# Output projection of a hybrid decoder layer: which block runs token-major, and in which order the blocks go

## The chip, the cores and the metric

One core of a Trainium2 chip. The metric is the device time of one execution in microseconds, the median of several runs. TensorE (PE, its weight loads PEld), VectorE (DVE), ScalarE (ACT), GpSimd (POOL) and SyncE (SP, which issues every DMA of this kernel) run side by side.

## The reference, cut to what matters

```
x: 2048 prompt tokens and 8 decode tokens, 2048 channels, float32
h    = RMSNorm(x) * (1 + scale) + shift
P    = h @ w_in                          -> u_a | v_a | z_a | x_b | z_b
y_a  = u_a * (tril(W_s) LN(v_a) + b_s) * SiLU(z_a)
y_b  = GLU(S5 state space of x_b) * SiLU(z_b)
o    = concat(y_a, y_b) @ w_out          (2048 x 2048)
out  = x + gate * RMSNorm(o) * g_post    (gate differs for prompt and decode rows)
```

The change touches the last two lines alone. RMSNorm needs the sum of squares over all 2048 channels of `o` before any output can be written.

## The kernel before, in words

Matrix products are made of three matmuls on float32r halves: each operand is split into a high and a low part (`split`, L87: a cast on ScalarE, L90, and a subtraction, L85), and high x high, low x high and high x low are summed in PSUM. Each matmul loads its own 128 x 128 stationary operand.

The 2056 tokens are four blocks of 512, the last with the 8 decode rows (`blk`). The input projection runs in two parts; in part two the order is block 3, 0, 1, 2. It leaves `y` in DRAM (`YA[b][h]`, by block, and `YB[e]`, by group of channels). Then comes the output projection, the subject here. Its stages are:

- `phase3` (L1137), channel-major, for blocks 0, 1 and 2: W_out is stationary, `y` (128 channels x 512 tokens) streams. There are 16 tiles of 128 output channels (n), each a sum over 16 row tiles (k). The first ng = 4 tiles share one pass over k, in which the `y` rows that aren't there yet are loaded (`yload`, L1085, six ahead; rows 8 to 15 come from `YB` in pieces of 256 bytes and are cast at L1098); then n = 4 to 15 one by one, with the next tile's W_out loaded meanwhile. `ev_o` (L1105) takes a finished tile out of PSUM: its square goes to a running sum (GpSimd, L1121), its value times the gate to SBUF.
- `phase3` for block 3, channel-major for its tokens 256 to 511 and the decode rows only: 264 columns per matmul, ng = 6.
- `phase3_rows` (L1228), token-major, for tokens 0 to 255 of block 3: `y` is stationary, W_out (128 x 512) streams; four quarters f of 512 channels, in each 16 k and two token tiles c. Here a token lies on a partition, so the sum of squares is per partition, and a token tile can be scaled as soon as it is complete. In the last quarter tile 1 runs LAG = 6 steps of k behind tile 0, so that tile 0's ending lies beside matmuls.

So W_out (16.8 MB) is read five times, each time in 32 pieces of 512 KB (`wraw`, L106), each split into two pairs of halves; `phase3_rows` asks for a piece four pieces ahead (`rows_w`, L1224).

The ending of a channel-major block (`final`, L1189) needs a sum over partitions (`rms_wide`, two matmuls with a matrix of ones), a reciprocal root on VectorE, and for each of 16 tiles a load of the residual (L1196, four buffers), a product (L1206), a sum (L1207) and a store (L1208). It is a generator: `finish_some` runs a step of it at given places of the next stage (k = 11, 13 and 15 of the first group, then once per tile). `gg_rows` (L1211) makes the gate as rows for the token-major stage: four activations and, in a later `turn`, a float32 matmul and a copy, four times; in block 3's channel-major part after n = 6, 8, 10 and 12. The token-major ending (`final` inside `phase3_rows`, L1237) is a chain of short VectorE instructions on 128 x 1 to the scale, then per quarter a fused multiply-add with the residual `xr` (L1254), one of the four on ScalarE and GpSimd instead (L1251, L1252), and a store (L1255).

All instructions are traced in written order; the framework then orders each engine's queue by priority and a simulated timeline, so transfers may be issued ahead of their written place, as far as buffers are free. `hl` has 32 buffers (16 rows of y, high and low), raw rows `t` six, raw pieces of W_out three, `o` tiles OB = 21.

Of the kernel before, what the change touches and what calls it, by code (L numbers as in the profile page):

```python
# [19 lines left out]
D = 2048  # L20
L = 2048
ND = 8
# [23 lines left out]
OB = 21  # L46
LAG = 6
NR_ = 8
XR0 = 41
OW = 2 * (TB // 2 + ND)  # L50

# [11 lines left out]
class Builder:  # L63
# [1041 lines left out]
    def ev_o(self, b, n, acc, rs, ssq, eng):  # L1105
        S, V = self.S, self.V
        if b < NB - 1 or n % 2 == 0:
            self.o2 = self.xp.tile([128, OW], F32, tag="o", bufs=OB, name=self.nm("o"))
        o = self.o2[:, n % 2 * (OW // 2) :] if b == NB - 1 else self.o2
# [12 lines left out]
        return o  # L1122
# [13 lines left out]

    def phase3(self, b, ws, y):  # L1137

        V, G, SP = self.V, self.G, self.SP
        rs = ranges(b) if b < NB - 1 else ranges(b)[1:]  # L1140
        c0 = rs[0][0]
        nn = rs[-1][0] + rs[-1][1] - c0
        ng = 4 if b < NB - 1 else 6
        ssq = self.xp.tile([128, TB + ND], F32, tag="ssq", bufs=2, name=self.nm("ossq"))
        kw = [{}, self.wkw]
        ws = [ws]
        acc = [[self.ps.tile([128, 512], F32, tag="acc" if g < 4 else "aux", bufs=4, name=self.nm("acc"))] for g in range(ng)]
# [12 lines left out]
        for g in range(ng):  # L1160
            self.finish_some(1)
            os_.append(self.ev_o(b, g, acc[g], rs, ssq, G))
        for n in range(ng, 16):
            ac = [self.ps.tile([128, 512], F32, tag="acc", bufs=4, name=self.nm("acc")) for _ in rs]
            nxt = []
            for k in range(KT):
                if k % 8 == 0 and n < 15:
                    nxt += self.wsplit(self.whalf(self.I["wout"][n + 1], k // 8), **(self.wkw if k else {}))
                self.kstep(ac, w, k, y[k], rs, k == 0, k == KT - 1)
                if k == 13:  # L1170
                    self.run_later()
                if n == 15 and b < NB - 1:
                    if k >= 4 and k % 2 == 0:
                        ynext.append(self.yload(b + 1, len(ynext)))
                    if k in (1, 9) or (k == 13 and b == NB - 2):
                        g = len(wnext)
                        wnext.extend(self.wsplit(self.wpair(self.I["wout"], g, 0), **kw[g // 4]))
                elif n == 15 and k in (1, 9):
                    wnext.append(self.rows_w(len(wnext)))
            self.finish_some(1 if n < 15 or b == NB - 1 else 16)  # L1180
            if b == NB - 1 and n % 2 == 0 and 6 <= n < 14:
                self.gg_rows((n - 6) // 2)
            os_.append(self.ev_o(b, n, ac, rs, ssq, G))
            w = nxt
        self.finish_some(16)
        self.finish = self.final(ssq, nn, os_, b * TB + c0, b * TB)
        return (y if b == NB - 1 else ynext), wnext

# [39 lines left out]
    def phase3_rows(self, b, y, ws):  # L1228

        V, G, S, T, SP = self.V, self.G, self.S, self.T, self.SP  # L1230
        ssq = self.sp_.tile([128, 2, 4], F32, name="ssqr")
        ws = dict(enumerate(ws))
        for i in range(len(ws), 4):
            ws[i] = self.rows_w(i)
        os_, xs = {}, {}
        mm = T.matmul
        def final(c):  # L1237

# [6 lines left out]
            self.rsqrt(r, v, t, h)  # L1245
            if c:
                V.tensor_mul(os_[c, 3], acc[c], self.ggr[3])
            for f in range(4):
                o, x = os_[c, f], xs[c, f]
                if f == 1 - c:  # L1250
                    S.activation(o, o, AF.Identity, scale=r)  # L1251
                    G.tensor_tensor(o, o, x, op=ALU.add)  # L1252
                else:
                    V.scalar_tensor_tensor(o, o, r, x, op0=ALU.mult, op1=ALU.add)  # L1254
                SP.dma_start(self.O["yr"][c * 128 : c * 128 + 128, f * 512 : f * 512 + 512], o)  # L1255
        for f in range(4):
            acc = [self.ps.tile([128, 512], F32, tag="acc", bufs=4, name=self.nm("acc")) for _ in range(2)]
            lag = LAG if f == 3 else 0
            held = []
            for k in range(KT + lag):  # L1260
                i = f * 8 + k // 2
                if k < KT and k % 2 == 0:
                    held += ws.pop(i)
                for c, kc in ((0, k), (1, k - lag)):
                    if not 0 <= kc < KT:
# [4 lines left out]
                    mm(acc[c], yh, wh, start=kc == 0, stop=False)  # L1270
                    mm(acc[c], yl, wh, start=False, stop=False)
                    mm(acc[c], yh, wl, start=False, stop=kc == KT - 1)
                    if kc == KT - 1:
                        sq = self.xp.tile([128, TB + ND], F32, tag="sq", bufs=2, name=self.nm("osq"))[:, 0:512]
                        os_[c, f] = self.xp.tile([128, OW], F32, tag="o", bufs=OB, name=self.nm("or"))[:, 0:512]
                        S.activation(sq, acc[c], AF.Square, accum_out=ssq[:, c, f : f + 1])
                        if (c, f) != (1, 3):
# [3 lines left out]
                if k < KT and k % 2:  # L1281
                    if i + 4 < 32:
                        ws[i + 4] = self.rows_w(i + 4)
                    if f or k >= 13:
                        self.finish_some(1)
                    if f * 16 + k >= XR0 and len(xs) < 8:
                        c, g = len(xs) // 4, len(xs) % 4
                        x = self.xp.tile([128, OW], F32, tag="o", bufs=OB, name=self.nm("xr"))[:, 0:512]
                        SP.dma_start(x, self.I["xr"][c][:, g * 512 : g * 512 + 512])
                        xs[c, g] = x  # L1290

# [85 lines left out]
    def build(self):  # L1377
# [108 lines left out]
        for b in (NB - 1, *range(NB - 1)):  # L1486
# [4 lines left out]
            else:  # L1491
                y0, ws0 = [], []
                raws = []
                def last(k):

                    if k == 1:
                        raws.extend(self.wraw(self.wpair(I["wout"], g, 0)) for g in (0, 2))
                    if k in (9, 14):
                        ws0.extend(self.wpieces(raws.pop(0)))
# [29 lines left out]
def layout(i):  # L1529
# [17 lines left out]
    out["woutr"] = i["w_out"].reshape(KT, 128, 4, 512).transpose(2, 1, 0, 3)  # L1547
    out["xr"] = x[(NB - 1) * TB : (NB - 1) * TB + NR].reshape(2, 128, D)
    out["ident"] = np.eye(128, dtype=np.float32)
# [23 lines left out]

NR = 256
OUTS = {"yT": (D, T - NR), "yr": (NR, D), "sav": (128, H, ND), "hp": (128, 2, 32), "hs": (128, 2, 32, ND)}


def unpack(r):
    t0 = (NB - 1) * TB
    yT = r["yT"].T  # L1580
# [16 lines left out]
```

## Time and profile before

| | |
|---|---|
| median of 3 runs | 2885.63 us (2882.94 to 2888.16) |
| profiled execution, device time | 2882.97 us |
| its span, first to last instruction | 2880.9 us |
| TensorE busy | 2817.2 us (98%), 15708 matmuls |
| weight loads / VectorE / ScalarE / GpSimd busy | 82% / 55% / 37% / 36% |
| DMA | 581.20 MB, 202 GB/s over the span |

A TensorE row's duration includes the passage through the array, so its pace is read from starts. Busy times are per stretch; `x` counts instructions that touch the stretch.

### The profile page before, as it was taken

What the parts mean: (1) busy time and instruction counts of PE and PEld (TensorE: products, weight loads), DVE (VectorE), ACT (ScalarE), POOL (GpSimd) and SP (SyncE); (2) the same over time, 40 slices, a digit from 0 to 9 for tenths busy, and PEclk for the clock granted to TensorE, in tenths of its full rate; (3) what the DMA queues carried; (4) which work ended last, traced back from release to release, by engine and by line L of the source; (5) the groups of instructions that cost most, each with busy time, mean ns of one, the idle gap of its engine ahead of it and who ended that gap; (6) DMA issues with size and microseconds to landing.
All of it is one profiled execution on the core that took longest, in us unless ns stands there. A gap on an engine that the chain in (4) does not pass through costs nothing.

```text
span 2880.9 us, 44125 instructions
## 1 busy us (share of the span) xinstructions
PE 2817.2 (98%) x15708; PEld 2365.8 (82%) x15708; DVE 1570.4 (55%) x2907; ACT 1062.2 (37%) x2008; POOL 1048.5 (36%) x973
## 2 busy tenths in 40 slices
PE   7999999999999999999999999999999999999998
PEld 4676777778899999988888888888888888888976
DVE  4467656465342837564647545573641273472866
ACT  3334444334233232423233332433243333434543
POOL 1128562662431233323232323233334355263442
PEclk9999999999999999999999999999999999999999
DMA  9898997987987373847475656646573355464676
GB/s 363 287 250 230 265 261 229 282 234 210 198 209 207 106 236 125 267 131 223 133 245 185 180 174 196 209 145 208 159 229 106 112 178 171 132 219 126 197 235 221
DMA packets 455167, 581.20 MB, mean 202 GB/s; under 512 B 216609, under 2 KB 303265, under 8 KB 454945
## 3 DMA queue, kind: packets, MB, share of 16 engines
q1 hardware_dynamic: 454946, 578.38, 66.9%
q8 instruction: 123, 2.02, 0.3%
q14 instruction: 98, 0.80, 0.1%
HBM read 466.94 MB, written 102.66 MB: 198 GB/s over the span
## 4 chain that ended last, share of the span: by engine, by line
PE 73%; DVE 14%; DMA 6%; issue 3%; POOL 1%; SPq 1%; ACT 1%; DVEq 0%; ACTq 0%; POOLq 0%
PE acc L97 21%; PE acc L99 20%; PE acc L98 20%; DVE Ub L943 3%; DVE wlo L85 2%; PE acc L655 2%; PE acc L656 2%; PE acc L657 2%; PE ada L271 1%; DMA wraw<-in_win 1%; DVE Ub L954 1%; DVE sct L953 1%; DVE sct L951 1%; DVE Ub L952 1%; DMA wraw<-in_woutr 1%
## 5 line engine op out<-in xcount | busy, mean ns | idle before, releaser
L85 DVE TENSOR_TENSOR wlo<-wraw,whi 128x512 fp32r<-128x512 f32 x626 | 544.6, 878 | 832.9 <-ACT whi L90 811.8
L90 ACT CAST whi<-wraw 128x512 fp32r<-128x512 f32 x960 | 580.4, 620 | 1101.3 <-PE acc L98 634.8
L97 PE MATMUL acc<-hi,whi 128*128 128x512 f32 (+2 forms) x2816 | 979.2, 349 | 1.4 <-ACT vtok L663 0.8
L99 PE MATMUL acc<-hi,wlo 128*128 128x512 f32 (+2 forms) x2816 | 968.7, 344 | 4.0 <-DVE wlo L85 3.9
L98 PE MATMUL acc<-lo,whi 128*128 128x512 f32 (+2 forms) x2816 | 968.2, 344 | 3.8 <-DVE lo L375 3.5
L85 POOL TENSOR_TENSOR wlo<-wraw,whi 128x512 fp32r<-128x512 f32 x334 | 472.7, 1418 | 1025.0 <-ACT whi L90 911.8
L97 PEld LDWEIGHTS acc<-hi,whi 128*128 128x128 f32 x2816 | 531.1, 189 | 82.2 <-issue 14.0
L99 PEld LDWEIGHTS acc<-hi,wlo 128*128 128x128 f32 x2816 | 530.4, 188 | 74.0 <-DVE wlo L85 6.1
L98 PEld LDWEIGHTS acc<-lo,whi 128*128 128x128 f32 x2816 | 531.1, 189 | 65.0 <-DVE lo L375 6.7
L97 PE MATMUL acc<-yhi,whi 128*128 128x512 f32 (+1 forms) x1024 | 377.3, 369 | 3.8 <-DVE o L1118 2.8
L99 PE MATMUL acc<-yhi,wlo 128*128 128x512 f32 (+1 forms) x1024 | 375.5, 368 | 2.1 <-POOL wlo L85 2.1
L98 PE MATMUL acc<-ylo,whi 128*128 128x512 f32 (+1 forms) x1024 | 376.1, 368 | 0.0
L97 PEld LDWEIGHTS acc<-yhi,whi 128*128 128x128 f32 x1024 | 193.5, 189 | 39.6 <-DVE o L1118 3.6
L99 PEld LDWEIGHTS acc<-yhi,wlo 128*128 128x128 f32 x1024 | 193.0, 189 | 36.7 <-POOL wlo L85 2.7
L98 PEld LDWEIGHTS acc<-ylo,whi 128*128 128x128 f32 x1024 | 193.5, 189 | 34.5 <-issue 0.7
L656 PE MATMUL acc<-wlo,hi 128*128 128x512 f32 x384 | 151.4, 394 | 0.0
L657 PE MATMUL acc<-whi,lo 128*128 128x512 f32 x384 | 151.1, 394 | 0.0
L655 PE MATMUL acc<-whi,hi 128*128 128x512 f32 x384 | 148.6, 394 | 0.0
L943 DVE SCALAR_TENSOR_TENSOR Ub<-Ub,apow 128x128 f32<-128x128 f32 (+6 forms) x384 | 146.3, 447 | 2.3 <-ACT Ub L930 2.0
L1032 POOL TENSOR_TENSOR sg<-sg,zbl 128x264 f32<-128x264 f32 x64 | 54.9, 858 | 195.5 <-DVE sg L1031 115.3
L90 ACT CAST hh<-hr 128x264 fp32r<-128x264 f32 x64 | 26.5, 414 | 194.6 <-DMA hr<-Ub 92.2
L1121 POOL TENSOR_TENSOR ossq<-ossq,osq 128x512 f32<-128x512 f32 (+1 forms) x60 | 81.5, 1358 | 35.3 <-ACT osq L1114 35.1
(295 smaller groups left out, 3137.6 us busy)
## 6 DMA issues: line engine op xcount, KB each, us to landing
wraw<-in_win SPq DMA_DIRECT2D x272, 512.0 KB
wraw<-in_wout SPq DMA_DIRECT2D x128, 512.0 KB
xr<-XB SPq DMA_DIRECT2D x128, 272.0 KB
x<-in_xT SPq DMA_DIRECT2D x128, 256.0 KB
wraw<-in_wss SPq DMA_DIRECT2D x64, 512.0 KB
wraw<-in_winv SPq DMA_DIRECT2D x48, 512.0 KB
XB<-t SPq DMA_DIRECT2D x64, 256.0 KB
wraw<-in_wgt SPq DMA_DIRECT2D x32, 512.0 KB
```

Of the source, the lines that this page charges most:

```text
L85: eng.tensor_tensor(out, a, b, op=ALU.subtract)
L90: self.S.copy(hi, raw)
L97: mm(acc, whi, xhi, start=start, stop=False)
L98: mm(acc, whi, xlo, start=False, stop=False)
L99: mm(acc, wlo, xhi, start=False, stop=stop)
L271: self.T.matmul(ps[k * 32 : k * 32 + 32, 0:256], self.stat[:, q * 4 + k, :], raw[:, k * 256 : k * 256 + 256], start=q == 0, stop=q == 3)
L655: mm(acc[c], hh, wh, start=k == 0, stop=False)
L656: mm(acc[c], hh, wl, start=False, stop=False)
L657: mm(acc[c], ho, wh, start=False, stop=k == KT - 1)
L943: V.scalar_tensor_tensor(o, i, f, o, op0=ALU.mult, op1=ALU.add)
L1032: self.G.tensor_tensor(sg, sg, zb, op=ALU.mult)
L1121: eng.tensor_tensor(ssq[:, 0:nn], ssq[:, 0:nn], sq[:, 0:nn], op=ALU.add)
```

## The change

Block 3 comes first and is channel-major as a whole: 256 + 264 columns, two PSUM banks per output tile, ng = 2, tiles in turn in the `acc` and `aux` banks. Blocks 0 and 1 follow as before. Block 2 comes last and is token-major as a whole: four token tiles with lags of 0, 2, 4 and 6 steps in the last quarter, `acc` and `aux` banks in turn by quarter. W_out is read four times. The first two pieces of W_out that are loaded ahead are now k = 0 to 7 of tiles 0 and 1 instead of k = 0 to 3 of tiles 0 to 3. In `phase3_rows` the finish of the block before starts at the third step and takes a step at each k; `gg_rows` runs at k = 10 to 13 of the first quarter. The low halves of W_out stay with VectorE and GpSimd in turn (before, in block 3, three of four on VectorE). Residual rows `xr` are 16 loads instead of 8, in buffers that other tiles leave free; the last four are loaded when tile 0 is finished.

```diff
-LAG = 6
+LAG = (0, 2, 4, 6)
...
-    def phase3(self, b, ws, y):
+    def phase3(self, b, ws, y, nb):
...
-        rs = ranges(b) if b < NB - 1 else ranges(b)[1:]
...
-        ng = 4 if b < NB - 1 else 6
+        rs = ranges(b)
+        nn = blk(b)
+        two = len(rs) == 2
+        ng = 2 if two else 4
...
+        def accs(n):
+            tag = "aux" if two and n % 4 > 1 else "acc"
+            return [self.ps.tile([128, 512], F32, tag=tag, bufs=4, name=self.nm("acc")) for _ in rs]
...
-            if k % 4 == 0 and k < KT - 4:
+            if k % 4 == 0 and k < KT - 4 and len(ws) == k // 4 + 1:
...
     def phase3_rows(self, b, y, ws):
...
+        NC = 4
...
+        room = {0: [("xres", 4)] * 4, 1: [("o", OB)] * 4, 2: [("fin", 2)] * 2 + [("ssq", 2)] * 2, 3: [("xres", 4)] * 4}
+        def xrow(c, g):
+            tag, n = room[c][g]
+            x = self.xp.tile([128, TB + ND], F32, tag=tag, bufs=n, name=self.nm("xr"))[:, 0:512]
+            SP.dma_start(x, self.I["xr"][c][:, g * 512 : g * 512 + 512])
+            xs[c, g] = x
...
-            for f in range(4):
+            for f in (range(4) if c < NC - 1 else (1, 0, 2, 3)):
                 o, x = os_[c, f], xs[c, f]
-                if f == 1 - c:
+                if f == 1 or (f == 3 and c < NC - 1):
                     S.activation(o, o, AF.Identity, scale=r)
                     G.tensor_tensor(o, o, x, op=ALU.add)
...
-            acc = [self.ps.tile([128, 512], F32, tag="acc", bufs=4, name=self.nm("acc")) for _ in range(2)]
-            lag = LAG if f == 3 else 0
+            acc = [self.ps.tile([128, 512], F32, tag="aux" if f % 2 else "acc", bufs=4, name=self.nm("acc")) for _ in range(NC)]
+            lag = LAG if f == 3 else (0,) * NC
...
+                while len(y) < min(KT, k + 6):
+                    y.append(self.yload(b, len(y)))
...
                     mm(acc[c], yh, wh, start=kc == 0, stop=False)
-                    mm(acc[c], yl, wh, start=False, stop=False)
-                    mm(acc[c], yh, wl, start=False, stop=kc == KT - 1)
+                    mm(acc[c], yh, wl, start=False, stop=False)
+                    mm(acc[c], yl, wh, start=False, stop=kc == KT - 1)
...
-                    if f or k >= 13:
-                        self.finish_some(1)
...
+                            if c == 0:
+                                for g in range(4):
+                                    xrow(3, g)
+                if k < KT and k % 2 and i + 4 < 32:
+                    ws[i + 4] = self.rows_w(i + 4)
+                if f * KT + k >= 2:
+                    self.finish_some(1)
+                if f == 0 and 10 <= k < 14:
+                    self.gg_rows(k - 10)
+                elif f == 0 and k > 11:
+                    self.run_later()
+                if f == 3 and 1 <= k < 13:
+                    xrow((k - 1) // 4, (k - 1) % 4)
...
-                        raws.extend(self.wraw(self.wpair(I["wout"], g, 0)) for g in (0, 2))
+                        raws.extend(self.wraw(self.wpair(I["wout"], 0, kq)) for kq in (0, 1))
...
-                        y0.append(self.yload(0, len(y0)))
+                        y0.append(self.yload(NB - 1, len(y0)))
...
-        for b in range(NB - 1):
-            y, ws = self.phase3(b, ws, y)
-        self.lo_engs = [V, V, V, G]
         self.ggr = []
-        y, ws = self.phase3(NB - 1, ws, y)
-        self.phase3_rows(NB - 1, y, ws)
+        todo = (NB - 1, *range(NB - 1))
+        for b, nb in zip(todo, todo[1:]):
+            y, ws = self.phase3(b, ws, y, nb)
+        self.phase3_rows(NB - 2, y, ws)
```

## Rows read from the trace of the kernel before

**Rows 1.** Table by stretch: blocks 0, 2, 3 channel-major, 3 token-major, tail; columns first.

```profile
core 0: us, PE busy (x) PEld busy (x) DVE busy (x) ACT busy (x) POOL busy (x), PEclk, DMA share, GB/s
2122.66:2300.70 178.04, 178.04 (x769) 144.22 (x768) 48.41 (x56) 71.62 (x118) 65.48 (x49) 1.00 0.44 137
...
2479.20:2657.70 178.50, 178.50 (x771) 144.58 (x770) 88.91 (x84) 67.56 (x113) 80.99 (x54) 1.00 0.54 165
2657.70:2766.60 108.90, 101.39 (x780) 97.96 (x779) 85.41 (x111) 59.36 (x126) 49.82 (x36) 0.97 0.71 219
2766.60:2869.30 102.70, 96.71 (x388) 74.26 (x386) 63.51 (x108) 40.87 (x81) 30.84 (x26) 0.95 0.69 216
2869.30:2880.90 11.60, 0.04 (x1) 0.00 (x0) 7.41 (x20) 2.02 (x4) 3.21 (x2) 0.66 0.52 182
```

**Rows 2.** The same table: input projection of block 3; block 1; block 3 channel-major.

```profile
860.00:900.00 40.00, 40.00 (x336) 40.00 (x335) 16.13 (x30) 12.21 (x29) 3.19 (x4) 1.00 0.86 233
2360.00:2380.00 20.00, 20.00 (x88) 16.18 (x87) 16.01 (x15) 5.55 (x10) 13.70 (x9) 1.00 0.84 267
...
2720.00:2740.00 20.00, 18.24 (x143) 17.34 (x142) 17.84 (x22) 9.84 (x23) 11.60 (x9) 1.00 0.91 304
```

**Rows 3.** TensorE in order of time: start, duration (us), instruction.

```profile
2122.66 0.39 PE L97 MATMUL acc<-yhi,whi 128*128 128x512 f32 x1
...
2657.83 0.28 PE L98 MATMUL acc<-ylo,whi 128*128 128x264 f32 x1
...
2661.94 0.28 PE L99 MATMUL acc<-yhi,wlo 128*128 128x264 f32 x1
...
2868.95 0.40 PE L1272 MATMUL acc<-wlo,yhi 128*128 128x512 f32 x1
```

**Rows 4.** Waits, both stretches of block 3: us in total, times, longest.

```profile
ACT whi L90 <- DMA wraw<-in_woutr: 56.7, 30, 5.0
...
ACT whi L90 <- DMA wraw<-in_wout: 39.6, 18, 6.7
```

**Rows 5.** Chain of waits in block 3: start us, us, what.

```profile
2726.77 4.63 DMA out_yT<-xres
2731.42 5.56 DMA xres<-in_xT
...
2777.13 3.69 DMA wraw<-in_woutr
```

**Rows 6.** Groups by form, block 3: count, busy us, mean ns, idle before and releaser.

```profile
L90 ACT CAST whi<-wraw 128x512 fp32r<-128x512 f32 x120 | 69.2, 618 | 102.3 <-DMA wraw<-in_woutr 56.7 <-DMA wraw<-in_wout 39.6 <-PE acc L99 3.2
...
L85 POOL TENSOR_TENSOR wlo<-wraw,whi 128x512 fp32r<-128x512 f32 x30 | 42.7, 1424 | 96.8 <-ACT whi L90 77.6 <-PE acc L1271 5.8 <-PE acc L1272 5.1
...
L1215 ACT ACTIVATE t<-c_ident,GG 128x128 f32<-128x128 f32 x16 | 5.1, 392 | 0.0
...
L1218 PE MATMUL ggr<-t,ones 128*128 128x512 f32 x8 | 4.2, 604 | 1.6 <-ACT t L1215 1.6
```

**Rows 7.** VectorE in order of time, y rows of block 0 becoming ready.

```profile
2140.36 3.23 DVE L85 TENSOR_TENSOR ylo<-t,yhi 128x512 fp32r<-128x512 f32 x3 [1.89 <-ACT yhi L1098]
...
2146.16 1.09 DVE L85 TENSOR_TENSOR ylo<-t,yhi 128x512 fp32r<-128x512 f32 x1
```

**Rows 8.** VectorE in order of time, the end of the kernel.

```profile
2865.98 0.69 DVE L1278 TENSOR_TENSOR or<-acc,t 128x512 f32<-128x512 f32 x1 [2.11 <-ACT osq L1276]
2866.59 0.15 DVE L1243 TENSOR_REDUCE fr_v<-ssqr 128x1 f32<-128x4 f32 x1
...
2869.08 2.08 DVE L1254 SCALAR_TENSOR_TENSOR or<-or,fr_r,xr 128x512 f32<-128x512 f32 x3
2871.08 0.15 DVE L1243 TENSOR_REDUCE fr_v<-ssqr 128x1 f32<-128x4 f32 x1
...
2874.05 3.08 DVE L1254 SCALAR_TENSOR_TENSOR or<-or,fr_r,xr 128x512 f32<-128x512 f32 x3
```

More of the change, by code (lines that the diff above doesn't have):

```diff
@@ L1106, in ev_o @@
         S, V = self.S, self.V
-        if b < NB - 1 or n % 2 == 0:
-            self.o2 = self.xp.tile([128, OW], F32, tag="o", bufs=OB, name=self.nm("o"))
-        o = self.o2[:, n % 2 * (OW // 2) :] if b == NB - 1 else self.o2
+        o = self.xp.tile([128, TB + ND], F32, tag="o", bufs=OB, name=self.nm("o"))
         sq = self.xp.tile([128, TB + ND], F32, tag="sq", bufs=2, name=self.nm("osq")) if n else ssq
@@ L1135, in wgroup @@
         return out
-    def phase3(self, b, ws, y):
-        V, G, SP = self.V, self.G, self.SP
-        rs = ranges(b) if b < NB - 1 else ranges(b)[1:]
-        c0 = rs[0][0]
-        nn = rs[-1][0] + rs[-1][1] - c0
-        ng = 4 if b < NB - 1 else 6
+    def phase3(self, b, ws, y, nb):
+        G = self.G
+        rs = ranges(b)
+        nn = blk(b)
+        two = len(rs) == 2
+        ng = 2 if two else 4
         ssq = self.xp.tile([128, TB + ND], F32, tag="ssq", bufs=2, name=self.nm("ossq"))
         kw = [{}, self.wkw]
-        ws = [ws]
-        acc = [[self.ps.tile([128, 512], F32, tag="acc" if g < 4 else "aux", bufs=4, name=self.nm("acc"))] for g in range(ng)]
+        def accs(n):
+            tag = "aux" if two and n % 4 > 1 else "acc"
+            return [self.ps.tile([128, 512], F32, tag=tag, bufs=4, name=self.nm("acc")) for _ in rs]
+        acc = [accs(g) for g in range(ng)]
         os_ = []
@@ L1163, in phase3 @@
         for n in range(ng, 16):
-            ac = [self.ps.tile([128, 512], F32, tag="acc", bufs=4, name=self.nm("acc")) for _ in rs]
+            ac = accs(n)
             nxt = []
@@ L1169, in phase3 @@
                 self.kstep(ac, w, k, y[k], rs, k == 0, k == KT - 1)
-                if k == 13:
-                    self.run_later()
-                if n == 15 and b < NB - 1:
+                if n == 15:
                     if k >= 4 and k % 2 == 0:
[L1174 to L1182, printed above, removed]
+                        ynext.append(self.yload(nb, len(ynext)))
+                    if k in (1, 9):
+                        if nb == NB - 2:
+                            wnext.append(self.rows_w(len(wnext)))
+                        else:
+                            wnext.extend(self.wsplit(self.wpair(self.I["wout"], len(wnext), 0), **kw[len(wnext) // 4]))
+            self.finish_some(1 if n < 15 else 16)
             os_.append(self.ev_o(b, n, ac, rs, ssq, G))
             w = nxt
-        self.finish_some(16)
-        self.finish = self.final(ssq, nn, os_, b * TB + c0, b * TB)
-        return (y if b == NB - 1 else ynext), wnext
+        self.finish = self.final(ssq, nn, os_, b * TB, b * TB if b < NB - 2 else (NB - 2) * TB)
+        return ynext, wnext if nb == NB - 2 else [wnext]
     def final(self, ssq, nn, os_, t0, out0):
@@ L1230, in phase3_rows @@
         V, G, S, T, SP = self.V, self.G, self.S, self.T, self.SP
-        ssq = self.sp_.tile([128, 2, 4], F32, name="ssqr")
+        NC = 4
+        ssq = self.sp_.tile([128, NC, 4], F32, name="ssqr")
         ws = dict(enumerate(ws))
@@ L1245, in final @@
             self.rsqrt(r, v, t, h)
-            if c:
+            if c == NC - 1:
                 V.tensor_mul(os_[c, 3], acc[c], self.ggr[3])
-            for f in range(4):
+            for f in (range(4) if c < NC - 1 else (1, 0, 2, 3)):
                 o, x = os_[c, f], xs[c, f]
-                if f == 1 - c:
+                if f == 1 or (f == 3 and c < NC - 1):
                     S.activation(o, o, AF.Identity, scale=r)
@@ L1256, in phase3_rows @@
         for f in range(4):
-            acc = [self.ps.tile([128, 512], F32, tag="acc", bufs=4, name=self.nm("acc")) for _ in range(2)]
-            lag = LAG if f == 3 else 0
+            acc = [self.ps.tile([128, 512], F32, tag="aux" if f % 2 else "acc", bufs=4, name=self.nm("acc")) for _ in range(NC)]
+            lag = LAG if f == 3 else (0,) * NC
             held = []
-            for k in range(KT + lag):
+            for k in range(KT + lag[-1]):
+                while len(y) < min(KT, k + 6):
+                    y.append(self.yload(b, len(y)))
                 i = f * 8 + k // 2
@@ L1263, in phase3_rows @@
                     held += ws.pop(i)
-                for c, kc in ((0, k), (1, k - lag)):
+                for c in range(NC):
+                    kc = k - lag[c]
                     if not 0 <= kc < KT:
@@ L1270, in phase3_rows @@
                     mm(acc[c], yh, wh, start=kc == 0, stop=False)
-                    mm(acc[c], yl, wh, start=False, stop=False)
-                    mm(acc[c], yh, wl, start=False, stop=kc == KT - 1)
+                    mm(acc[c], yh, wl, start=False, stop=False)
+                    mm(acc[c], yl, wh, start=False, stop=kc == KT - 1)
                     if kc == KT - 1:
                         sq = self.xp.tile([128, TB + ND], F32, tag="sq", bufs=2, name=self.nm("osq"))[:, 0:512]
-                        os_[c, f] = self.xp.tile([128, OW], F32, tag="o", bufs=OB, name=self.nm("or"))[:, 0:512]
+                        os_[c, f] = self.xp.tile([128, TB + ND], F32, tag="o", bufs=OB, name=self.nm("or"))[:, 0:512]
                         S.activation(sq, acc[c], AF.Square, accum_out=ssq[:, c, f : f + 1])
-                        if (c, f) != (1, 3):
+                        if (c, f) != (NC - 1, 3):
                             V.tensor_mul(os_[c, f], acc[c], self.ggr[f])
@@ L1280, in phase3_rows @@
                             final(c)
-                if k < KT and k % 2:
-                    if i + 4 < 32:
-                        ws[i + 4] = self.rows_w(i + 4)
-                    if f or k >= 13:
-                        self.finish_some(1)
[L1286 to L1290, printed above, removed]
+                            if c == 0:
[11 more added lines that the diff above has]
+                    xrow((k - 1) // 4, (k - 1) % 4)
     def startup(self, st, NG, ntl):
@@ L1547, in layout @@
     out["woutr"] = i["w_out"].reshape(KT, 128, 4, 512).transpose(2, 1, 0, 3)
-    out["xr"] = x[(NB - 1) * TB : (NB - 1) * TB + NR].reshape(2, 128, D)
+    out["xr"] = x[(NB - 2) * TB : (NB - 1) * TB].reshape(4, 128, D)
     out["ident"] = np.eye(128, dtype=np.float32)
@@ L1571, in layout @@
     return {k: A(v) for k, v in out.items()}
-NR = 256
+NR = TB
 OUTS = {"yT": (D, T - NR), "yr": (NR, D), "sav": (128, H, ND), "hp": (128, 2, 32), "hs": (128, 2, 32, ND)}
 def unpack(r):
-    t0 = (NB - 1) * TB
+    t0 = (NB - 2) * TB
     yT = r["yT"].T
```

4 lines of the change are left out of this document (1 added, 3 removed).

## The prediction

> **What bounds the kernel now.** I read the table by stage first. Its rows [rows 1] cut the output projection into five stretches, between the first TensorE instruction of each block, and a tail. In the first (block 0) and the third (block 2) TensorE is busy without a break, 178.04 of 178.04 us and 178.50 of 178.50 us; block 1 has the same 178.5 us. In the two stretches of block 3 it isn't: the channel-major one lasts 108.9 us with 101.4 us busy, the token-major one 102.7 us with 96.7 us busy, and the granted clock falls to 0.97 and 0.95, which means moments on the lower level (1.2 GHz instead of 2.4). So the kernel is bound by TensorE up to block 3, and there by something that keeps TensorE waiting.
>
> Next I took the time of one matmul from starts, since a row's duration includes the pipeline. A 512-column one takes 178.5/768 = 0.2324 us [rows 1]. 264-column ones start 35 in a row from 2657.83 to 2661.94 us: 4.11/34 = 0.121 us [rows 3]. Alternating 256 and 264 columns, the shape that block 3 has in the input projection, 335 fit into 40.00 us: 0.1194 us on average, at a granted clock of 1.00 [rows 2]. The unhindered time of block 3 is thus 768 x 0.121 = 92.9 us and 384 x 0.2324 = 89.2 us. It loses 108.9 - 92.9 = 16.0 us and 102.7 - 89.2 = 13.5 us, **29.5 us together**.
>
> The table of waits says what is late [rows 4]: over both stretches ScalarE, which casts a piece of W_out to its high part, stands 56.7 us before pieces from in_woutr and 39.6 us before pieces from in_wout, waiting for the transfer. The chain of waits names the same and a helper [rows 5]: transfers of W_out of 3.7 us one after the other, and, from 2726.77, a store of the finished block 2 (4.63 us) and a load of its residual (5.56 us) that stand in the same SyncE queue as W_out. The reason is the rate: a 512 KB piece feeds 24 matmuls of 264 columns (24 x 0.121 = 2.9 us) or 12 of 512 (2.8 us), some 180 to 190 GB/s for W_out alone, while in a block of 512 tokens it lasts 24 x 0.2324 = 5.6 us (94 GB/s). Where the residual and the stores of the block before run beside the slow rate, the DMA engines are 0.91 busy at 304 GB/s and TensorE has 18.24 us of 20; beside the rate of a whole block they are 0.84 busy at 267 GB/s and TensorE has 20.00 of 20 [rows 2].
>
> **The change, part by part.** *Matmuls.* Block 3 now takes 1536 of 256 and 264 columns: 1536 x 0.1194 = 183.4 us. Blocks 0 and 1 keep 178.5 us each, the sum over channels of the block before (two short matmuls) included as now. Block 2 token-major has 768 of 512 columns, 178.5 us. Its scale rows (the four turns of `gg_rows`) move from block 3 into its first quarter: TensorE is busy 4.2 us with them in either place [rows 6]. The stages sum to 183.4 + 178.5 + 178.5 + 182.7 = 723.1 us, against 178.0 + 178.5 + 178.5 + 108.9 + 102.7 = 746.6 us now: **-23.5 us**. The matmuls alone would be 1.3 us dearer (183.4 for 92.9 + 89.2); all of the gain is the 29.5 us lost, less the 4.2 us of the turns, which stay.
>
> *A rule against it.* A 264-column matmul with its own load of 128 weights starts every 0.121 us [rows 3], and its columns alone need 264/2.4 GHz = 0.110 us, so the load is nearly hidden. The Trainium skill, page "TensorE: Matmul & The Clock Gate", Part 3, section "The mechanism", says that a weight load overlaps a running matmul only when the two use different row groups; all of these use all 128 rows, and its 107 ns for a load (an estimate from P/1.2 on the same page) times 384 added loads would be +41 us. The trace speaks against that rule here, and the sum goes by the rows.
>
> *W_out.* 32 of 160 pieces go, with 64 casts at 618 ns on ScalarE and 64 subtractions, 1424 ns each on GpSimd [rows 6]. That work lies beside TensorE's and counts only through the stalls above. The low halves are now shared evenly by VectorE and GpSimd in the last block, where three in four went to VectorE; one GpSimd subtraction per piece of 5.6 us is covered. The new order in the token-major stage wants a low half one matmul (0.23 us) earlier, under four pieces of lead: nothing.
>
> *Start of the stage.* This is where the change adds a wait. Block 0 now takes a row of y each 2.8 us (12 matmuls), and four channel tiles share it; block 3 takes one each 12 x 0.1194 = 1.43 us, with two tiles. From TensorE's first matmul of the stage, 2122.66 [rows 3], y row 13 is wanted at 2141.3 and row 15 at 2144.2. VectorE finishes rows 11 to 13 at 2143.6 and row 15 at 2147.25 now [rows 7]: 2.3 and 3.1 us late. I take **+3**; below, nothing (the loads can be ordered better, as nothing forced them now), above +10, since the decode rows add a small transfer and split to eight of them, on ScalarE, VectorE and SyncE, and behind each stands the next one.
>
> *Entry of the token-major stage.* Its y rows come during the last channel tile before, as for blocks 1 and 2, which lose nothing [rows 1]. The finish of block 1 (a residual load, two elementwise steps and a store per tile) begins at k = 2 instead of 11, beside W_out at 94 GB/s; the second row of [rows 2] is that company, with no loss. Queued behind it on SyncE are the W_out pieces, with a lead of four pieces, 22 us, against 11 now. The scale rows need 16 short ScalarE activations (5.1 us), and TensorE waited 1.6 us for them [rows 6]; four in a row can wait again. **+2** in all, bounds 0 and +6. The eight more residual loads and stores of `yr` replace the transposed ones of the finish; the bytes are equal.
>
> *Tail.* Now, after the last matmul (starts 2868.95 [rows 3], ends about 2869.3), 11.6 us pass [rows 1]. VectorE sets them: for the first token tile a product (0.69), the chain to its scale (2866.59 to 2869.08, 2.49) and three fused steps in 2.08; only then, at 2871.08, the last tile's chain (2.97 with its product) and its three steps (3.08), to 2877.13; then the stores land, 3.8 us [rows 8]. After, four tiles end with lags of 0, 2, 4 and 6, so 45, 24 and 9 matmuls or 10.4, 5.6 and 2.1 us before the last. Tiles 0 to 2 cost VectorE 0.69 + 2.49 + 2 x 0.7 = 4.6 us each, tile 3 6.05. VectorE can start 1 us after a tile's end: tile 0 at -9.4, tile 1 at -4.5, tile 2 at +0.1, tile 3 at +4.7, ending at +10.7 and with the stores at +14.5: +2.9. With the fused steps at 1.03 us, as they are beside GpSimd, and the square of tile 2 late on ScalarE, it is +5.5; with 0.7 throughout +1.6. I take **+3.5**.
>
> Sum: -23.5 + 3 + 2 + 3.5 = **-15.0 us**. The profiled execution took 2882.97 us, so 2868.0; it lay 2.7 us under the median of the three runs (2885.63), and against that the number is **2870.6**. The bounds give -23.5 + 0 + 0 + 1.6 = -21.9 (2863.7) and -23.5 + 10 + 6 + 5.5 = -2.0 (2883.6). About 0.2% (5.8 us) is what a measurement of this kernel can tell from no change.
>
> **The rivals.**
> - *Not W_out, but the finish of the block before is what stops TensorE.* For it: the store and the residual load in the chain [rows 5]. Against: the same finish beside a whole block, no loss [rows 2]. Place: the first third of the token-major stage, where a finish of 16 full tiles now stands ahead of W_out in SyncE's queue from k = 2. If it decides, which it does once W_out is later than its lead of 22 us, the lost 25.3 us (29.5 - 4.2) are lost again: stages 748.4, +1.8, with start and tail +8.3: **2893.9, slower**. Chance 0.08.
> - *Half of each.* 12.6 us come back: **2883**, no change that can be told. Chance 0.08.
> - *The y rows pace the first group.* If they come only each 2.8 us, as they are used now, its 16 steps take 20 us more, 17 beyond the 3 counted: **2888**. Against: the times of [rows 7], where eight strided rows are done within 20 us of the other transfers. Chance 0.06.
> - *The weight loads show.* The load records fill 40.00 of 40.00 us in the narrow stretch [rows 2]; if 384 more of them were on the path at their share of it, 0.119 us, they would cost 46 us: **2916**. (The Trainium skill's rule above would have this effect.) Against: the same stretch's own pace. Chance 0.02.
>
> **How the numbers follow.** The forecast has 0.76, nearly all of it faster by over 0.2%; "half of each" straddles the edge. Faster 0.76, same 0.14 (half, y rows, the worst end of the forecast), slower 0.10. The range, 2862 to 2883, is the forecast's own with both bounds; what lies outside is the finish, the y rows and the loads, 0.16.
>
> **What would show it.** Right: W_out waits of ScalarE no longer followed by idle TensorE, its granted clock 1.00 through the last stage but for the tail; block 3 in some 186 us, the last stage in some 185, a tail of about 15. Wrong: gaps of TensorE in the first 60 us of the token-major stage with SyncE at a residual load (first rival); a first group of block 3 well over 26 us (third); pairs of 256 and 264 columns over 0.24 us apart (fourth).

## The result, and the profile after

The changed kernel takes 2869.9 us (median of 4 runs, 2865.27 to 2871.85), the kernel before beside it 2884.44 us: ratio 0.995, 95% interval 0.9937 to 0.9964, **faster by 14.5 us**. The forecast was 2870.6 us. The profiled execution took 2870.61 us with a span of 2868.7.

First the table by stretch of the changed kernel, cut as in [rows 1]: block 3 (channel-major as a whole), block 0, block 1, block 2 (token-major), tail.

```profile
2125.03:2310.00 184.97, 184.57 (x1537) 184.16 (x1536) 51.32 (x79) 77.05 (x157) 64.78 (x49) 1.00 0.44 133
2310.00:2488.70 178.70, 178.70 (x774) 144.79 (x773) 90.24 (x88) 67.87 (x116) 80.35 (x55) 1.00 0.55 165
2488.70:2667.30 178.60, 178.60 (x772) 144.62 (x771) 91.42 (x85) 67.94 (x114) 82.72 (x55) 1.00 0.54 164
2667.30:2851.10 183.80, 182.69 (x779) 145.67 (x777) 83.62 (x118) 59.93 (x118) 53.81 (x38) 1.00 0.49 149
2851.10:2868.70 17.60, 0.00 (x0) 0.00 (x0) 13.04 (x34) 3.96 (x7) 7.71 (x5) 0.65 0.64 229
```

Granted clock 1.00 in all four stages; TensorE stands still for 0.4 us in the first and 1.1 us in the last. Block 3 takes 185.0 us for the 211.6 of [rows 1], of which 4.2 us were the scale rows that went to block 2; the DMA share of its stages fell from 0.71 and 0.69 to 0.44. In sum, against the profiled execution before: the stages 726.1 for 746.7 us (-20.6), the tail 17.7 for 11.6 (+6.1; from here on counted from the end of the last matmul to the end of the span), and the projection begins at 2125.03 for 2122.66 (+2.4). Up to rounding that is the -12.2 us between the spans, 2868.7 and 2880.9.

The table of waits of the changed kernel (us in total, times, longest): the first line over the whole projection, the others over the token-major stage.

```profile
ACT whi L88 <- DMA wraw<-in_wout: 115.6, 39, 8.9
...
ACT whi L88 <- DMA wraw<-in_woutr: 39.4, 9, 10.4
...
PE acc L1275 <- DVE ylo L83: 1.1, 1, 1.1
```

ScalarE still waits 39.4 us for W_out in the last stage, where [rows 4] had 56.7 us. But TensorE's only wait there is for a low half of y. **The length of a wait on an engine with a lead says nothing about the end; whether the engine after it waits too, does.** The name of TensorE's wait can still mislead: in the kernel before, its recorded waits in block 3 sum to 13.3 us, and only 4.1 of them are for halves of W_out. How W_out's lateness comes under another name is shown below.

Of block 3's pace, TensorE in order of time, with the one wait of its first group:

```profile
2146.43 0.86 PE L95 MATMUL acc<-yhi,whi 128*128 128x256 f32 x5 [0.37 <-ACT yhi L1096]
...
2179.80 0.29 PE L97 MATMUL acc<-yhi,wlo 128*128 128x264 f32 x1
...
2185.91 0.28 PE L97 MATMUL acc<-yhi,wlo 128*128 128x256 f32 x1
```

From 2179.80 to 2185.91 lie 51 starts: 6.11/51 = 0.1198 us each, and 1536 of them are 184.0 us. The stage's other 1.0 us is lost around this wait, between 2145.8 and 2147.8, where y rows come late.

### The profile page after: what moved, and what is told of

It reads as the page before. It is cut to its first block, busy times and chain, and to the rows that moved or that the text cites. A ratio compares the mean times of both kernels' runs of the same rounds, so it can differ in the third digit from the quotient of the medians.

```text
span 2868.7 us, 44543 instructions
## 1 busy us (share of the span) xinstructions
PE 2811.1 (98%) x16092; PEld 2381.8 (83%) x16092; DVE 1514.9 (53%) x2847; ACT 1029.7 (36%) x1965; POOL 1025.7 (36%) x953
## 4 chain that ended last, share of the span: by engine, by line
PE 77%; DVE 12%; DMA 5%; issue 2%; SPq 2%; ACT 1%; POOL 1%; DVEq 0%; ACTq 0%; POOLq 0%
PE acc L95 20%; PE acc L97 20%; PE acc L96 19%; DVE Ub L941 3%; PE acc L1275 2%; PE acc L1273 2%; PE acc L1274 2%; DVE wlo L83 2%; DMA wraw<-in_win 2%; PE acc L653 2%; PE acc L654 2%; PE acc L655 2%; PE ada L269 1%; DVE Ub L952 1%; DVE sct L951 1%
## 5 line engine op out<-in xcount | busy, mean ns | idle before, releaser
L88 ACT CAST whi<-wraw 128x512 fp32r<-128x512 f32 x896 | 545.6, 620 | 1081.7 <-PE acc L96 611.3
L83 DVE TENSOR_TENSOR wlo<-wraw,whi 128x512 fp32r<-128x512 f32 x564 | 489.1, 872 | 832.6 <-ACT whi L88 801.5
L96 PE MATMUL acc<-ylo,whi 128*128 128x512 f32 (+2 forms) x1024 | 346.0, 338 | 0.0
L97 PE MATMUL acc<-yhi,wlo 128*128 128x512 f32 (+2 forms) x1024 | 346.0, 338 | 0.0
L95 PE MATMUL acc<-yhi,whi 128*128 128x512 f32 (+2 forms) x1024 | 345.0, 338 | 0.4 <-ACT yhi L1096 0.4
L97 PEld LDWEIGHTS acc<-yhi,wlo 128*128 128x128 f32 x1024 | 192.4, 188 | 22.6
L1275 PE MATMUL acc<-whi,ylo 128*128 128x512 f32 x256 | 100.0, 395 | 1.1 <-DVE ylo L83 1.1
L1274 PE MATMUL acc<-wlo,yhi 128*128 128x512 f32 x256 | 100.9, 394 | 0.0
```

The source lines that it names most:

```text
L83: eng.tensor_tensor(out, a, b, op=ALU.subtract)
L88: self.S.copy(hi, raw)
L95: mm(acc, whi, xhi, start=start, stop=False)
L96: mm(acc, whi, xlo, start=False, stop=False)
L97: mm(acc, wlo, xhi, start=False, stop=stop)
L1274: mm(acc[c], yh, wl, start=False, stop=False)
```

## The experiments

Lengths in us, each stage from its first matmul to the next stage's first, the last one to the end of its last matmul. Each ratio is against runs of the kernel before that were taken beside it (medians 2884.44 to 2886.01). Two medians of one kernel can differ by a few us because the part ahead of the projection does (last section), so the stages decide where a few us matter.

| run | built on | channel-major part of block 3 | token-major stage | tail | time (95% interval of the ratio to before) |
|---|---|---|---|---|---|
| before | | 108.9 | 102.8 | 11.6 | 2884.44 |
| b_no_finish | before | 99.7 | 97.3 | 11.9 | 2875.68 (0.9956 to 0.9981) |
| b_half_w | before | 98.9 | 89.5 | 11.7 | 2862.4 (0.9906 to 0.9935) |
| b_half_load | before | 108.6 | 89.5 | 11.4 | 2870.39 (0.993 to 0.9963) |
| b_half_split | before | 105.7 | 90.7 | 12.1 | 2872.16 (0.9937 to 0.9967) |
| after | | (all: 185.0) | 183.8 | 17.7 | 2869.9 (0.9937 to 0.9964) |
| a_tail_order | after | | 184.3 | 18.4 | 2872.29 (0.9935 to 0.9964) |
| a_tail_joint | after | | 184.0 | 16.7 | 2869.88 (0.9919 to 0.9952) |
| a_double_w | after | | 206.5 | 18.1 | 2896.71, one run |
| a_finish_late | after | | 182.2 | 17.7 | 2868.75, one run |
| c_tail_alone | after | | 183.8 | 14.8 | 2865.81 (0.9914 to 0.9955) |
| c_alone_late | after | | 182.3 | 14.8 | 2864.1 (0.9913 to 0.9949) |

### What block 3 lost before: W_out, or the endings of blocks 2 and 3

Four runs on the kernel before. **b_no_finish** leaves out the endings of block 2, which ran beside block 3's channel-major part, and of block 3's own channel-major tokens, which ran beside the token-major part: the sum over partitions, scaling, residual and stores. So these rows of the output are not written.

```diff
-        self.finish = self.final(ssq, nn, os_, b * TB + c0, b * TB)
+        self.finish = self.final(ssq, nn, os_, b * TB + c0, b * TB) if b < NB - 2 else None
```

> The kernel before, without the ending of blocks 2 and 3 in its channel-major parts (no residual load, no scale, no sum, no store for them); the output projection's matmuls and all W_out pieces stay. TensorE now loses 29.5 us in the two stretches of block 3, 4.2 us of it the scale rows. If the rate at which W_out pieces are wanted (one per 2.8 us) makes the loss, most of it stays: time 2 to 10 us below the kernel before. If the ending of the block before, which shares SyncE's queue and the DMA engines, makes it, the loss goes to 5 to 10 us: time 18 to 26 us below.

**b_half_w** takes pieces of W_out in block 3 from the piece before, neither loaded nor split: 13 of 32 in the channel-major part and every second one in the token-major part, "half" below; **b_half_load** skips only the load, **b_half_split** only the cast and the subtraction. So nearly half the products of block 3 are formed with a neighbour's weights. The helper of the first; in the second the raw piece is held and split each time, in the third the raw piece is loaded each time and, where the halves are taken again, not used:

```diff
+    def wone(self, src, again, slot, **kw):
+        if not again:
+            self.got[slot] = self.wsplit(src, **kw)
+        return self.got[slot]
...
-        return self.wsplit(...)
+        return self.wone(..., i % 2 == 1, 2, ...)
```

> The kernel before, with every second piece of W_out in block 3's two stretches neither loaded nor split (the piece before it is used again, so block 3's output is of the wrong weights); the ending of the blocks before stays. W_out's rate as the cause: the loss of 29.5 us falls to 5 to 12 us, time 16 to 24 us below the kernel before. The ending as the cause: 0 to 6 us below.

> As the run with half the pieces, but only the loads are halved: each loaded piece is split a second time (cast on ScalarE, subtraction on VectorE or GpSimd) where the next one would be. If the transfers of W_out bind, as the waits of ScalarE for them say: like the run with half the pieces, 14 to 24 us below the kernel before. If the splitting binds (engines busy, queues in order): 0 to 6 us below.

> The other half: all pieces of W_out are loaded in block 3, every second one is not split (the halves of the piece before are used again). Transfers bind: 0 to 6 us below the kernel before. Splitting binds: 14 to 24 us below.

In whole times the runs lie 9.3, 22.6, 14.6 and 12.9 us under the kernel before: the first two as expected of W_out's rate, the third at the low end of what was expected of the transfers, the fourth between its two ranges. The stages tell more. Table by stretch, the channel-major and the token-major part of block 3; in order b_no_finish, b_half_w, b_half_load, b_half_split:

```profile
2659.90:2759.60 99.70, 98.05 (x777) 95.35 (x776) 47.91 (x77) 61.49 (x131) 34.97 (x30) 1.00 0.59 179
2759.60:2856.90 97.30, 93.11 (x386) 72.25 (x384) 42.70 (x67) 37.98 (x75) 21.32 (x17) 0.98 0.56 169
```

```profile
2663.40:2762.30 98.90, 97.94 (x780) 95.37 (x779) 70.30 (x96) 48.73 (x107) 42.88 (x33) 1.00 0.66 198
2762.30:2851.80 89.50, 89.50 (x388) 72.14 (x386) 37.84 (x78) 20.28 (x41) 14.62 (x15) 1.00 0.41 125
```

```profile
2664.40:2773.00 108.60, 102.54 (x779) 98.87 (x778) 88.87 (x114) 60.37 (x131) 51.97 (x37) 0.97 0.58 166
2773.00:2862.60 89.60, 89.57 (x388) 72.17 (x386) 59.75 (x103) 39.83 (x75) 29.78 (x25) 1.00 0.48 143
```

```profile
2662.10:2767.80 105.70, 99.52 (x779) 96.74 (x778) 64.83 (x94) 47.74 (x105) 40.33 (x32) 0.98 0.80 252
2767.80:2858.50 90.70, 90.08 (x388) 71.99 (x386) 40.00 (x81) 20.30 (x44) 15.24 (x16) 1.00 0.65 208
```

Against the unhindered 92.9 and 89.2 us, before loses 16.0 and 13.6. Half of W_out leaves 6.0 and 0.3: 23.3 of the 29.6 us come back. Without the ending 6.8 and 8.1 are left: 14.7 come back. The two sum to 38, more than the loss, so they are not two separate shares: part of it needs both, and either's going frees it. One place that needs both is in the rows of the kernel before, ScalarE and then TensorE:

```profile
2793.50 1.14 ACT L90 CAST whi<-wraw 128x512 fp32r<-128x512 f32 x2 [2.77 <-DMA wraw<-in_woutr]
2794.55 0.41 ACT L90 CAST sqh<-ossq 128x264 fp32r<-128x264 f32 x1
```

```profile
2795.01 0.59 PE L158 MATMUL ssum<-sqh,ones 128*128 128x264 f32 x1 [3.85 <-ACT sqh L90]
```

This is TensorE's longest wait in block 3, for the sum of squares of the ending; ScalarE makes it ready only after two casts of W_out, for which it had waited 2.77 us.

The two parts of block 3 also differ. In the token-major one, half the loads alone or half the splits alone end the loss (0.3 and 1.5 left). In the channel-major one neither does (15.7 and 12.8 left). There the 20 us stretches show a second limit. One stretch each of before, b_half_split and b_no_finish, at the same place of the stage (fourth column VectorE):

```profile
2697.70:2717.70 20.00, 17.22 (x121) 16.87 (x121) 19.90 (x24) 12.10 (x30) 15.50 (x12) 0.83 0.51 159
```

```profile
2702.10:2722.10 20.00, 16.74 (x127) 16.74 (x128) 19.86 (x28) 8.47 (x21) 13.18 (x10) 0.91 0.60 203
```

```profile
2699.90:2719.90 20.00, 20.00 (x167) 20.00 (x166) 9.41 (x18) 13.29 (x30) 11.08 (x11) 1.00 0.62 213
```

VectorE is busy for 19.90 of 20 us and the DMA share is only 0.51: here the ending's products and sums, W_out's subtractions and the eviction of finished tiles fill VectorE. TensorE is busy for 17.22 us, at a granted clock of 0.83, so some of them at the lower of its two levels. Without the ending VectorE has 9.41 us and TensorE all 20. A full VectorE alone doesn't stop TensorE, though, as the same place in b_half_load shows:

```profile
2704.40:2724.40 20.00, 20.00 (x159) 19.34 (x158) 19.51 (x24) 12.58 (x31) 16.68 (x13) 1.00 0.26 79
```

Nor are VectorE's 19.90 us all work. VectorE, then GpSimd, in the kernel before:

```profile
2698.34 0.68 DVE L85 TENSOR_TENSOR wlo<-wraw,whi 128x512 fp32r<-128x512 f32 x1
...
2702.93 1.77 DVE L85 TENSOR_TENSOR wlo<-wraw,whi 128x512 fp32r<-128x512 f32 x1
```

```profile
2702.42 1.73 POOL L85 TENSOR_TENSOR wlo<-wraw,whi 128x512 fp32r<-128x512 f32 x1
```

The same subtraction takes 0.68 us, and 1.77 us where it begins during a step of GpSimd; then it ends at 2704.70, 0.55 us after that step (2704.15). All eleven VectorE steps over 0.9 us in this stretch end 0.55 us after one of GpSimd's. Counted at 0.69 us each they are some 8 us shorter (an estimate from these rows): so much of the 19.90 is standing still beside GpSimd, the effect that the tail shows below.

The waits of TensorE go the same way, in the channel-major part of b_half_load and then of b_half_split:

```profile
PE acc L100 <- DVE wlo L86: 5.6, 4, 2.8
```

```profile
PE acc L98 <- DVE o L1119: 4.7, 1, 4.7
```

With full splits they are for VectorE's low half of W_out, with half of them for VectorE's eviction. So W_out's rate was the larger cause, as a transfer and as splitting; the endings were its partner, with 9.2 us back in the channel-major part and 5.5 in the token-major one. What the splitting costs through VectorE's own work, and what through its standing still beside GpSimd, no run separates.

### Does the rate of W_out decide in the new stage too, and does the ending

**a_double_w** loads and splits each piece twice in the token-major stage, the first copy unused; **a_finish_late** starts the ending of block 1 at the twelfth step instead of the third.

```diff
     def rows_w(self, i):
+        self.wsplit(self.I["woutr"][i // 8][...], ...)
         return self.wsplit(self.I["woutr"][i // 8][...], ...)
```

> The changed kernel with every W_out piece of the token-major stage loaded and split twice, the first copy unused: one piece per 2.8 us again, as in block 3 before, beside the ending of a block and all other work of that stage. If that rate is what kept TensorE waiting, the stage of 183.8 us grows by 10 to 35 us and its granted clock falls below 1.00. If the place of the scale rows or the shape of the stage made the gain, it grows by less than 3 us.

```diff
-                if f * KT + k >= 2:
+                if f * KT + k >= 11:
                     self.finish_some(1)
```

> The changed kernel with the ending of block 1 begun at step 11 of the token-major stage instead of step 2. TensorE idles 1.26 and 0.40 us at 2702 and 2714 us now, the first wait on VectorE's subtraction for a y row, in the 20 us in which VectorE is 9.97 and 10.00 of 10 us busy with the ending. If the early start is the cause, these waits go and the stage falls from 183.8 to about 182 us. If not, it stays within 0.4 us.

The token-major stage by stretch, in a_double_w and in a_finish_late:

```profile
2670.20:2876.70 206.50, 192.46 (x779) 148.58 (x777) 125.11 (x148) 92.62 (x177) 96.11 (x67) 0.97 0.65 204
```

```profile
2667.10:2849.30 182.20, 182.20 (x779) 145.82 (x777) 79.23 (x118) 60.08 (x118) 53.04 (x38) 1.00 0.50 146
```

W_out at the rate that block 3 had before costs 22.7 us (206.5 for 183.8), TensorE stands still for 14.0 us of the stage and its granted clock is 0.97 again. An ending nine steps later gives back 1.6 us, and TensorE is busy throughout: its early start was the cause of the 1.1 us wait for y, and no more hangs on it.

### The tail

The tail was 2.6 us longer than forecast. My first idea was the order in VectorE's queue, where the steps of tiles 1, 2 and 3 lie mixed. **a_tail_order** keeps the written order there from the last step on.

```diff
+                if f == 3 and k == KT - 1:
+                    cm = self.tc.manual_schedule(engines={V.engine})
+                    cm.__enter__()
...
+        cm.__exit__(None, None, None)
```

> The changed kernel with VectorE's instructions kept in written order from the first token tile's ending on: one tile's product, scale chain and fused steps before the next tile's. The changed kernel's tail is 17.6 us after the last matmul, 2.5 more than forecast; its VectorE queue has the short steps of one tile's chain between the 512-wide steps of another. If that order is the cause, the tail falls to 14 to 15.5 us. If SyncE's queue of twelve stores and the four late residual loads sets the tail, it stays at 17 to 18.

**a_tail_joint** keeps that order and makes one chain of 128x2 steps for tiles 2 and 3 in place of two of 128x1.

```diff
-            v = self.sp_.tile([128, 1], F32, name=self.nm("fr_v"))
...
+            if c == NC - 2:
+                return
+            c0, w = (c, 1) if c < NC - 2 else (c - 1, 2)
+            v = self.sp_.tile([128, w], F32, name=self.nm("fr_v"))
...
```

> As the run with the written order, and the scale chain of the last two token tiles made once, on 128 x 2, when the last is complete. VectorE as the bound of the tail: one chain of 2.5 us less, tail 11.5 to 13.5 us. Stores as the bound: 16 to 18, since all eight of the last two tiles now come at the end.

The order was not it: 18.4 us, more than either idea had it. The joint chain gave 1.7 against that run and 1.0 against the changed kernel; 16.7 us is what was expected if the stores were the bound, so this run alone did not tell. What both left is in the rows. VectorE, then GpSimd, in order of time, in the changed kernel (start us, us, instruction):

```profile
2852.04 2.42 DVE L1254 SCALAR_TENSOR_TENSOR or<-or,fr_r,xr 128x512 f32<-128x512 f32 x2
...
2854.45 1.15 DVE L141 TENSOR_TENSOR fr_t<-fr_r 128x1 f32<-128x1 f32 x1
...
2857.14 1.41 DVE L1254 SCALAR_TENSOR_TENSOR or<-or,fr_r,xr 128x512 f32<-128x512 f32 x2
2858.47 1.22 DVE L142 SCALAR_TENSOR_TENSOR fr_t<-fr_t,fr_v 128x1 f32<-128x1 f32 x1
2859.72 1.19 DVE L143 SCALAR_TENSOR_TENSOR fr_r<-fr_t,fr_r 128x1 f32<-128x1 f32 x1
2860.94 0.16 DVE L141 TENSOR_TENSOR fr_t<-fr_r 128x1 f32<-128x1 f32 x1
...
2861.52 3.08 DVE L1254 SCALAR_TENSOR_TENSOR or<-or,fr_r,xr 128x512 f32<-128x512 f32 x3
```

```profile
2852.56 3.02 POOL L1252 TENSOR_TENSOR or<-or,xr 128x512 f32<-128x512 f32 x2 [3.92 <-DMA out_yr<-or]
2857.93 2.96 POOL L1252 TENSOR_TENSOR or<-or,xr 128x512 f32<-128x512 f32 x2 [2.35 <-ACT or L1251]
```

A step of 128x1 takes 0.16 us alone and 1.15 to 1.22 beside GpSimd's adds, and it ends with them: 2854.45 + 1.15 = 2855.60 and 2859.72 + 1.19 = 2860.91 against 2852.56 + 3.02 = 2855.58 and 2857.93 + 2.96 = 2860.89. The same in a_tail_order, VectorE and GpSimd (2854.97 + 1.18 = 2856.15 against 2853.66 + 2.48 = 2856.14):

```profile
2854.00 0.94 DVE L141 TENSOR_TENSOR fr_t<-fr_r 128x1 f32<-128x1 f32 x1
2854.97 1.18 DVE L142 SCALAR_TENSOR_TENSOR fr_t<-fr_t,fr_v 128x1 f32<-128x1 f32 x1
2856.19 0.16 DVE L143 SCALAR_TENSOR_TENSOR fr_r<-fr_t,fr_r 128x1 f32<-128x1 f32 x1
```

```profile
2853.66 2.48 POOL L1252 TENSOR_TENSOR or<-or,xr 128x512 f32<-128x512 f32 x2 [3.94 <-DMA out_yr<-or]
```

And a_tail_joint, where the five last fused steps take 1.28 us each on average beside three of GpSimd's adds:

```profile
2860.09 6.41 DVE L1258 SCALAR_TENSOR_TENSOR or<-or,fr_r,xr 128x512 f32<-128x512 f32 x5
```

```profile
2860.40 4.89 POOL L1256 TENSOR_TENSOR or<-or,xr 128x512 f32<-128x512 f32 x3 [2.42 <-ACT or L1255]
```

If that is the cause, GpSimd's help is the loss, though each add takes a step off VectorE. **c_tail_alone** takes the help away from tiles 1 to 3, so that VectorE has two more fused steps for tile 1 and three more for tiles 2 and 3. Against a_tail_joint:

```diff
-                if f == 1 or (f == 3 and cc < NC - 1):
+                if cc == 0 and f % 2:
                     S.activation(o, o, AF.Identity, scale=rr)
                     G.tensor_tensor(o, o, x, op=ALU.add)
```

> The joint ending of token tiles 2 and 3 as in the run before it, but ScalarE and GpSimd help with the first token tile only; the other twelve fused steps are all VectorE's. Theory: GpSimd's adds of 512 elements are what stretches VectorE's short steps (0.16 to 1.1 us) and fused steps (0.70 to over 1.0 us). Then the 128x2 steps of the scale take 0.15 to 0.25 us, eight fused steps 0.70 us each, and the tail is 0.7 + 2.5 + 5.6 + 4 and 0.6 ahead = 13.4 us, at most 15; the whole 2 to 3 us under the joint ending. Rival: the eight stores at the very end (8 x 256 KB behind one SyncE queue) set it; then the tail is 16.5 us or more whatever VectorE does. Second rival: the two more fused steps on VectorE cost what GpSimd's going gives back: 16 to 17 us.

VectorE at its end, and SyncE's stores:

```profile
2850.86 0.16 DVE L141 TENSOR_TENSOR fr_t<-fr_r 128x2 f32<-128x2 f32 x1
...
2852.51 0.69 DVE L1250 TENSOR_TENSOR or<-acc,t 128x512 f32<-128x512 f32 x1
2853.11 5.38 DVE L1258 SCALAR_TENSOR_TENSOR or<-or,fr_r,xr 128x512 f32<-128x512 f32 x8
```

```profile
2847.59 11.26 SPq L1259 DMA_DIRECT2D out_yr<-or  x12
```

Eight fused steps in 5.38 us, where five took 6.41: 0.67 each. The tail is 14.8 us, 1.9 under the joint ending; the whole went down by 4.1, of which the start of the projection in these medians is a part that I don't count. SyncE issues the last store at 2858.85, 0.36 us after VectorE's last step, so its queue does not hold the stores back. But the DMA engines (last but one column) are now full beside and behind VectorE's last steps:

```profile
2854.50:2860.50 6.00, 0.00 (x0) 0.00 (x0) 3.99 (x7) 0.00 (x0) 0.00 (x0) 0.50 1.00 342
```

Whether a still faster VectorE would shorten this tail further is therefore not shown.

The Trainium skill, page "SBUF — State Buffer", section "Who interferes with whom", says that a VectorE instruction with two SBUF inputs and a GpSimd instruction that reads SBUF exclude each other, and that the later one waits until the other is finished. The steps of lines L141 to L143 and the fused steps have two such inputs, and the rows agree: the stretched short steps that are worked out above end within 0.02 us of GpSimd's adds. One step with a single input was held too: in a_tail_joint the TENSOR_SCALAR of L139 on 128x2 took 1.11 us beside an add, in c_tail_alone 0.17. The rule on two inputs doesn't cover it, and no run here was made for it.

### The best of both

**c_alone_late** is c_tail_alone with the late ending.

> The same with the finish of block 1 from the twelfth step on instead of the third. The late finish gave 1.6 us in the token-major stage (182.2 for 183.8), so that stage should take 182.2 to 182.6 us, the tail 13.4 to 15, and the whole 2863 to 2866 us, 4 to 6 under the changed kernel (ratio to the kernel before 0.992 to 0.994). If the two gains do not add, because the late finish's stores meet something later, the stage is 184 again and the whole 2866 to 2868.

Its token-major stage and tail by stretch:

```profile
2663.40:2845.70 182.30, 182.26 (x779) 145.85 (x777) 82.32 (x117) 59.91 (x118) 53.76 (x38) 1.00 0.50 147
2845.70:2860.40 14.70, 0.00 (x0) 0.00 (x0) 10.35 (x26) 0.69 (x2) 0.00 (x0) 0.58 0.77 273
```

The two gains add: 1.5 and 2.9 us in the stages, **4.4 us** under the changed kernel. The whole is 2864.1 us (ratio 0.9931, 0.9913 to 0.9949), 5.8 under; the intervals of the two ratios overlap, so the 4.4 of the stages is the firmer number.

## Why the prediction was right

Its sum, -15.0 us, met the measured -14.5. That it did so to half a us is luck: the stages gave -20.6 us for the -18.5 of its terms, the tail +6.1 for +3.5, and these two errors cancel. The mechanism, W_out's rate, was right.

- *W_out's rate is what block 3 loses* (-23.5): right. Half of it gives 23.3 us back in the kernel before, twice of it costs 22.7 in the kernel after. But the reason given, the transfer, was too narrow: in the channel-major part half the loads alone gave 0.3 us back and half the splits alone 3.2, both together 10.0.
- *Matmul pace*: 0.1194 was forecast, 0.1198 measured, 184.0 us for 183.4. The weight loads do not show. By the Trainium skill's rule in "TensorE: Matmul & The Clock Gate", Part 3, section "The mechanism", that a load overlaps a running matmul only where the row groups differ, the 384 more loads would have cost +41 us (the forecast's estimate from that page); the stage of 185.0 us refutes it for this kernel. The same section of the Trainium skill has a second case that the prediction left out: a load into the background weight buffer is pulled ahead of running matmuls, too; which case these loads are, no run here shows.
- *Start of the stage* (+3, bounds 0 and +10): about +1.0, with one recorded wait of 0.37 us. The bound "the loads can be ordered better, as nothing forced them now" was the nearer end; the y rows cost this once and pace nothing after it.
- *Entry of the token-major stage* (+2, beside 4.2 for the scale rows): right in size. The stage is 183.8 us for 184.7. The late ending leaves 182.2, so the early one costs 1.6; the four turns of scale rows took the rest, 182.2 - 178.5 = 3.7, and TensorE didn't wait for them.
- *Tail* (+3.5): **mis-sized**, +6.1. The forecast let VectorE run its chains at the 2.49 us of a chain alone, and put GpSimd's price only on the fused steps, as its upper end (+5.5). The runs showed that the chain's steps stand still beside GpSimd too, up to 1.2 us each. With the help confined to tile 0 and one chain less (c_tail_alone) it was 14.8 us.
- *No term for the time ahead of the projection*: its work is not touched, yet the stage began 2.4 us later in the profiled execution. This lies within what its start varies by (last section).
- *Rivals*. "The finish stops TensorE": half right for the kernel before (14.7 us go with it) and wrong for the one after, where a later one gives 1.6. "Half of each" came nearest to the cause in the kernel before, but not to the time after: with the rate down, the early ending cost 1.6 us and no more. "The y rows pace the first group" and "the weight loads show" fell.

## What to carry to other kernels

Two loads that each fit beside the matmuls may not fit together: take either away and half of the loss or more goes, so removing one alone is no measure of its share, and halving it one resource at a time tells more. Look for VectorE steps that take far longer than the same form elsewhere, at a kernel's end above all, and at what GpSimd does in that moment: a VectorE that seems full may be standing still in part, and an add handed to GpSimd that blocks VectorE for as long as VectorE would have needed for it is no help. An engine's wait counts only when the next engine on the path waits as well.

## What was not expected of the hardware

That a VectorE step of one element per partition can take 1.2 us, seven times its usual 0.16, beside GpSimd, and that the same effect fills VectorE in the middle of the kernel before (both above).

And that the work ahead of the projection varies by more than most steps here are worth. The projection began at 2121.38 us in the profiled execution of c_tail_alone and at 2127.68 in that of a_tail_joint, with the same work in the same order ahead of it. Part of it comes up between 700 and 900 us; a_tail_joint, then c_tail_alone (second column TensorE's busy time and its instructions, seventh the granted clock):

```profile
700.00:900.00 200.00, 190.70 (x1607) 184.75 (x1606) 76.71 (x162) 60.54 (x145) 63.05 (x99) 0.97 0.85 199
```

```profile
700.00:900.00 200.00, 193.38 (x1648) 187.70 (x1647) 79.41 (x170) 62.86 (x150) 64.33 (x100) 0.99 0.87 205
```

TensorE stands still for 9.3 and 6.6 us there, at DMA shares of 0.85 and 0.87. What makes the difference wasn't settled. It is why a change of some us is read from its stage and not from one time.
